# A new source order in a decoder trunk: softmax behind its scores, a projection between scores and scaling, transposes behind the next projection

## The chip, the cores and the metric

The kernel runs on one core of one Trainium2 chip. The metric is the device time of one execution in microseconds, as the median of several runs. The profile shows one execution: TensorE (PE, with its weight loads PEld), VectorE (DVE), ScalarE (ACT), GpSimd (POOL) and the DMA queues, of which SyncE (SP) issues most.

## The reference

A decoder trunk of two layers, 512 tokens of width 1024, all in float32. Layer 0 mixes with a gated DeltaNet (6 heads of 128), layer 1 with sliding-window attention (12 query heads, 2 key heads of width 64, window 128, a sink logit per head). Each layer also attends with 4 heads into 256 fixed memory tokens, and ends in a SwiGLU block of width 2816.

```python
for layer in range(2):
    h = rms_norm(x, ln_mix[layer])
    mem_k, mem_v = split(mem_n @ w_mem_kv[layer])
    if layer == 0:   # q, k, v: projection, causal convolution of 4 taps, SiLU
        mix_out, mem_q = gated_deltanet_mixer(h, ...)
    else:
        proj = h @ swa_w_q
        mix_out = sliding_window_attention(rope(proj[:, :768]), shared_k, shared_v, sinks)
        mem_q = proj[:, 768:]
    mem_o = memory_attention(mem_q, mem_k, mem_v)       # softmax(q k / 8) v
    x = x + concat([mix_out, mem_o]) @ w_out[layer]
    x = x + swiglu(rms_norm(x, ln_ffn[layer]), w_gate_up[layer], w_down[layer])
    if layer == 0: shared_k, shared_v = split(rms_norm(x, ln_kv) @ w_kv)
return rms_norm(x, ln_final)
```

The DeltaNet runs in 4 chunks of 128 tokens here: within a chunk a triangular system is inverted, and a state of 128 x 128 per head is carried from chunk to chunk.

## The kernel before

Activations lie transposed, features on the 128 partitions and 512 tokens along the free axis, in eight tiles. Each float32 operand of a projection is split into a rounded high part and a low rest (`split`, L166: ACT copies `hi`, DVE subtracts to get `lo`), and a projection of 128 outputs (`project`, L199) is 8 x 3 = 24 matmuls of 128 x 512. Its weights are loaded by SP into `wraw` (2 buffers), then split into `whi` on ACT and `wlo` on DVE (3 buffers).

Stages in order: `mem_and_norm` and `gates` (to about 48 us), `gdn` (to about 281 us, with the first output products mixed in), output projection and SwiGLU of layer 0 (to about 660 us), `swa` (to about 781 us), output projection and SwiGLU of layer 1.

The Python source issues the instructions. When the program is built, a planner gives every engine its fixed queue: it works through the program with estimated durations and lets an engine take, among the instructions that it then thinks ready, the one that stands first in the source. So an engine's queue isn't the source order, but the source order decides who goes first; on the chip each engine then works through its queue in order and waits where an input is late. `nosync` (L114) adds an order between two instructions of one engine. `use` (L120) switches ACT's function table (`LN_EXP` for Exp and Ln, `SILU_SIN` for SiLU) behind all users of the former table.

`gdn` (L454): for each of 6 heads, `conv_tile` (L444) projects a key tile into a PSUM bank `pj` (3 banks), ACT copies it with one tap's gain and DVE adds three more taps; then SiLU, 4 transposes on PE into a bank `g`, a copy to `kg` and 4 squares (L473 to L486). Products of keys follow (L502), the gate projections, two memory queries `qm`, and the inversion of 32 x 32 blocks on DVE (`base_inverse`, L613: 31 steps of two operations, `btmp` and `big`). Then two passes (L544): memory attention of one query tile, three query heads projected and convolved, SiLU, products with the keys. Then `solve` (L652), `values` (L562: projection, convolution, SiLU, transposes, per head) and `scan` (L575: four chunks, heads inside; `scan_step`, L678, with PSUM banks `sc`), for heads 0 to 2 and then 3 to 5, and `finish` (L582: norm and gate, which make the operands of the output projection).

Attention: `scores(q, k)` (L710) makes, for two blocks of 128 queries at a time, 8 score matmuls into a bank pair (`qk` in layer 1, one pair), takes maxima on DVE (for windows with the mask, into tiles `sm`), and for memory tiles also the exponentials. `weigh` (L748) computes for windows the exponentials (14 on ACT, L767) with their sums `den`, then the reciprocal (L770), scales the probabilities (`sm`, half of the blocks on ACT, half on DVE), transposes them on PE into `pt` (in layer 0 into `g`), copies them to `pf`, multiplies with the values into `sc`, and splits the result into the operand of the output projection. A `nosync` (L790) puts the first transpose of a tile behind the last score matmul issued before it.

`swa` (L1064) orders 8 tiles, 6 and 7 being memory queries: two projections, keys, values, `score(6)`, then `queries(0)`, `score(7)`, `weigh(6)`, and the loop L1127: next tile's query, this tile's scores, last tile's `weigh`.

Of the kernel before, what the change touches and what calls it, by code (L numbers as in the profile page):

```python
# [9 lines left out]
F32 = mybir.dt.float32  # L10
# [76 lines left out]
class Builder:  # L87
# [366 lines left out]
    def gdn(self, gp):  # L454
# [15 lines left out]
        N = [every[:, h * NC:(h + 1) * NC, :] for h in range(H)]  # L470
        ss = self.t(gp, [P, NH], F32, "ss")
        self.weng = nc.vector
        for h in range(H):  # L473
            k = self.conv_tile(H + h, self.t(gp, [P, T], F32, f"kn{h}"))
            self.fn(k, k, AF.Silu)
            kn.append(k)
            ps = self.bank("g")
            for c in range(NC):
                self.tr(ps[:, chunk(c)], k[:, chunk(c)])
            t = c4(self.t(gp, [P, T], F32, f"kg{h}"))  # L480
            self.copy(t, c4(ps))
# [54 lines left out]
            h, c = divmod(i, NC)  # L536
            self.copy(kg[h][:, c, :], kg[h][:, c, :], scale=f[:, 2, i:i + 1])

        def memory(m):
            self.use(LN_EXP)  # L540
            self.attention(gp, qm[m], self.memK[m], self.memV, m, mq[m])


        for h0 in (0, 3):  # L544
            memory(h0 // 3)
            ts = [self.conv_tile(h, self.t(gp, [P, T], F32, "qv", 5)) for h in range(h0, h0 + 3)]
            self.use(SILU_SIN)
# [12 lines left out]
        vt = []  # L560

        def values(heads):  # L562
            for h in heads:
                v = self.conv_tile(2 * H + h, self.t(gp, [P, T], F32, "qv", 5))
                self.fn(v, v, AF.Silu)
                ps = self.bank("g")
                for c in range(NC):
                    self.tr(ps[:, chunk(c)], v[:, chunk(c)])
                self.tt(nc.vector, N[h], c4(ps), wide(ir[h]), ALU.mult)
                vt.append(N[h])  # L570
# [1 line left out]

        S = [None] * H

        def scan(heads):  # L575
            for c in range(NC):
                for h in heads:
                    S[h] = self.scan_step(gp, h, c, S[h], kn[h], Tt[h], kg[h], vt[h], qg[h], AT[h], br[h])

# [22 lines left out]
        for heads in (first, second):  # L602
            self.solve(gp, heads, [N[h] for h in heads], X, [Tt[h] for h in heads])
        values(first)
        scan(first)
        values(second)
        self.use(LN_EXP)
        scan(second)
        finish(first)
# [94 lines left out]
        return new  # L704


    def attention(self, pool, q, kk, vv, m, out, sinks=None):
        self.weigh(pool, self.scores(pool, q, kk, sinks is not None), vv, m, out, sinks)

    def scores(self, pool, q, kk, win):  # L710

        nc = self.nc
        own = "pt" in self.pbufs
        half = [slice(0, 64), slice(64, P)]
        sm = [self.t(pool, [P, 2, 2, 2 * P], F32, "sm", 4 if own else 2) for _ in range(2)]
        sm = [t[:, n] for t in sm for n in range(2)]
        mx = self.t(pool, [P, 2 * NC], F32, "mx", 2)
        den = self.t(pool, [P, 2 * NC], F32, "den", 2)
        nm = self.t(pool, [P, 2 * NC], F32, "nm", 2)
        for n0 in range(0, NC, 2):  # L720
            if own:
                two = self.bank("qk", [P, 2, 2, 2 * P])
                ps = [two[:, b] for b in range(2)]
            else:
                ps = [self.bank("sc" if n0 else "g", [P, 2, 2 * P]) for _ in range(2)]
            for n in (n0, n0 + 1):
                ks = slice((n - 1) * P if n else 0, (n + 1) * P) if win else slice(0, ML)
                c0 = P if win and n == 0 else 0
                for b in range(2):
                    self.scored = self.mm(ps[b][:, n - n0, c0:], q[half[b], n * P:(n + 1) * P], kk[half[b], ks])  # L730
            for b in range(2):
                i = b * NC + n0
                if win:
                    for n in (n0, n0 + 1):
                        c0 = 0 if n else P
                        nc.vector.tensor_tensor_reduce(  # L736
                            out=sm[n][:, b, c0:], in0=ps[b][:, n - n0, c0:], in1=self.band[:, c0:], scale=1.0,
                            scalar=NEG, op0=ALU.add, op1=ALU.max, accum_out=mx[:, b * NC + n:b * NC + n + 1])
                else:
                    nc.vector.tensor_reduce(out=mx[:, i:i + 2], in_=ps[b], op=ALU.max, axis=AX.X)  # L740
                    self.ts(nm[:, i:i + 2], mx[:, i:i + 2], -0.125, ALU.mult)
                    for n in (n0, n0 + 1):
                        i = b * NC + n
                        self.fn(sm[n][:, b, :], ps[b][:, n - n0, :], AF.Exp, scale=0.125, bias=nm[:, i:i + 1],
                                accum_out=den[:, i:i + 1])
        return sm, mx, den, nm

    def weigh(self, pool, scores, vv, m, out, sinks):  # L748

        nc = self.nc  # L750
        win = sinks is not None
        own = "pt" in self.pbufs
        half = [slice(0, 64), slice(64, P)]
        sm, mx, den, nm = scores
        if win:
            sk = sinks.unsqueeze(2).to_broadcast([P, 2, NC])
# [11 lines left out]
                            accum_out=den[:, i:i + 1])  # L768
            self.tt(nc.vector, den, den, es, ALU.add)
        nc.vector.reciprocal(den, den)  # L770
        o = self.bank("sc")
        group = NC if own else 2
        for n in range(NC):
            if n % group == 0:
                pf = {}
            k0 = 1 if win and n == 0 else 0
            p = sm[n][:, :, k0 * P:]
            dn = den.rearrange("p (b n) -> p n b", b=2)[:, n, :]
            for b in range(2):
                if n % 2:  # L780
                    self.copy(p[:, b], p[:, b], scale=dn[:, b:b + 1])
                else:
                    self.ts(p[:, b], p[:, b], dn[:, b:b + 1], ALU.mult)
            pt = self.bank("pt" if own else "g", [P, 2, 2, P])
            for j in range(k0, 2):
                for b in range(2):
                    turned = self.tr(pt[:, j, b, :], sm[n][:, b, j * P:(j + 1) * P])
                    if own and self.scored is not None:

                        self.nosync(turned, self.scored)  # L790
                        self.scored = None
            pf[n] = self.t(pool, [P, 2, 2, P], F32, "pf", group)
            if own and n == 2:
                nc.vector.tensor_copy(pf[n][:, k0:], pt[:, k0:])
            else:
                self.copy(pf[n][:, k0:], pt[:, k0:])
# [267 lines left out]
    def swa(self, sp):  # L1064
# [41 lines left out]
        def score(t):  # L1106
            got[t] = self.scores(sp, qs[t], kk[0] if t < 6 else memK[t - 6], t < 6)

        def weigh(t):
            mix[t] = self.pair(self.bpool)  # L1110
            if t < 6:
                self.weigh(sp, got[t], vv, t, mix[t], sinks[:, t, :])
            else:
                self.weigh(sp, got[t], memV, t - 6, mix[t], None)

        got = {}
        queries(6)
# [1 line left out]
        keys()  # L1119
        values()  # L1120
        score(6)
        transpose_values()
        queries(0)
        score(7)
        weigh(6)
        last = 7
        for t in range(6):  # L1127
            if t < 5:
                queries(t + 1)
            score(t)  # L1130
            weigh(last)
            last = t
        weigh(last)
        return [mix[t] for t in range(KD)]
# [88 lines left out]
```

## Time and profile before

| | |
|---|---|
| median of 3 runs | 1165.34 us (1165.07 to 1167.91) |
| the profiled execution | 1165.44 us, its span 1163.7 us |
| PE busy | 1139.6 us (98%), 7476 matmuls |
| DVE busy | 843.7 us (73%) |
| ACT busy | 635.8 us (55%) |
| PE in the chain that ended last | 88% |

A row of the timeline has start, duration, engine, line, operation, tile written and tiles read, shape and count; in square brackets the engine's idle time just before and what ended it. A row of the sums has the stretch, its length, busy time and number of instructions of PE, PEld, DVE, ACT and POOL, the granted clock, the busy share of the DMA engines and GB/s; for one tile the engines that don't touch it are left out. Matmuls are pipelined: a record is longer than the distance to the next one's start, so gaps are read from start to start.

### The profile page before, as it was taken

To read this page: it belongs to the slowest core of one execution; us is meant where nothing else is said; L and a number is where in the kernel's file an instruction comes from. 1 tells how busy PE (TensorE), PEld (TensorE's weight loads), DVE (VectorE), ACT (ScalarE), POOL (GpSimd) and SP (SyncE) were. 2 spreads that over 40 slices of the span, in tenths; PEclk is the share of its full clock that TensorE was granted. 3 is DMA by queue.
4 is the path that set the end of the run, shared out by engine and by line. 5 is a ranking of instruction groups with operands and counts; after the bars stand their busy time and mean duration, and the time that the engine had idled before them with its cause. 6 is when DMAs were issued, how large, how long until landed. Compare 5 with 4: busy or idle time off the path is not lost.

```text
span 1163.7 us, 19670 instructions
## 1 busy us (share of the span) xinstructions
PE 1139.6 (98%) x7476; PEld 997.3 (86%) x7476; DVE 843.7 (73%) x1587; ACT 635.8 (55%) x1273; POOL 85.9 (7%) x97
## 2 busy tenths in 40 slices
PE   7999999999999999999999999999999999999996
PEld 6888777877899998899998777678999988999986
DVE  5754877767789887378866767859799843898754
ACT  7569563366556652256654547675566522566533
POOL 0310000000101100011100000010011100111000
PEclk9999999999999999999999999999999999999998
DMA  8434352224657744567723421143477733577232
GB/s 307 135 101 115 113 127 92 74 90 163 170 142 187 183 127 124 148 148 179 182 70 102 136 73 38 55 107 124 106 187 185 186 108 103 141 182 187 70 93 94
DMA packets 73971, 152.83 MB, mean 131 GB/s; under 512 B 17756, under 2 KB 18420, under 8 KB 73876
## 3 DMA queue, kind: packets, MB, share of 16 engines
q1 hardware_dynamic: 62356, 130.59, 36.2%
q0 software_dynamic: 11520, 20.98, 11.7%
q8 instruction: 59, 0.97, 0.4%
q14 instruction: 36, 0.29, 0.1%
HBM read 144.58 MB, written 6.96 MB: 130 GB/s over the span
## 4 chain that ended last, share of the span: by engine, by line
PE 88%; DVE 7%; ACT 2%; DMA 1%; issue 1%; SPq 0%; DVEq 0%; ACTq 0%
PE pj L144 42%; PE g L144 39%; PE sc L144 5%; DVE wlo L151 2%; PE pt L148 1%; PE g L148 1%; ACT whi L138 1%; ACT sm L132 1%; DMA wraw<-in_wmk 1%; DVE sm L736 0%; DVE l L154 0%; DVE l L151 0%; PE qk L144 0%; DMA wraw<-in_win 0%; DVE q L151 0%
## 5 line engine op out<-in xcount | busy, mean ns | idle before, releaser
L138 ACT ACTIVATE whi<-wraw 128x512 fp32r<-128x512 f32 (+2 forms) x331 | 244.9, 746 | 272.5 <-PE pj L144 179.3
L151 DVE TENSOR_TENSOR wlo<-wraw,whi 128x512 fp32r<-128x512 f32 (+2 forms) x331 | 274.1, 837 | 108.3 <-ACT whi L138 102.4
L144 PE MATMUL pj<-h,whi 128*128 128x512 f32 (+1 forms) x676 | 266.1, 395 | 0.2
L144 PE MATMUL pj<-l,whi 128*128 128x512 f32 (+1 forms) x676 | 265.0, 392 | 0.3 <-DVE l L154 0.3
L144 PE MATMUL pj<-h,wlo 128*128 128x512 f32 (+1 forms) x676 | 265.0, 392 | 0.0
L144 PE MATMUL g<-T,whi 128*128 128x256 f32 x1280 | 232.1, 282 | 0.0
L144 PEld LDWEIGHTS g<-T,whi 128*128 128x128 f32 x1280 | 196.8, 189 | 1.5 <-DVE fu L154 1.5
L144 PE MATMUL g<-T,wlo 128*128 128x256 f32 x640 | 180.1, 281 | 0.0
L144 PEld LDWEIGHTS pj<-h,whi 128*128 128x128 f32 x676 | 127.0, 188 | 29.3 <-issue 3.1
L144 PEld LDWEIGHTS pj<-l,whi 128*128 128x128 f32 x676 | 127.0, 188 | 27.5 <-issue 2.0
L144 PEld LDWEIGHTS pj<-h,wlo 128*128 128x128 f32 x676 | 127.2, 188 | 26.6 <-issue 1.9
L144 PE MATMUL g<-h,wlo 128*128 128x256 f32 (+1 forms) x508 | 146.5, 288 | 0.0
L144 PE MATMUL g<-h,whi 128*128 128x256 f32 (+1 forms) x508 | 146.3, 288 | 0.0
L144 PE MATMUL g<-l,whi 128*128 128x256 f32 (+1 forms) x508 | 146.1, 288 | 0.0
L144 PEld LDWEIGHTS g<-T,wlo 128*128 128x128 f32 x640 | 120.4, 188 | 0.0
L144 PEld LDWEIGHTS g<-h,wlo 128*128 128x128 f32 x508 | 96.5, 190 | 1.2 <-issue 0.2
L144 PEld LDWEIGHTS g<-l,whi 128*128 128x128 f32 x508 | 96.5, 190 | 1.3
L144 PEld LDWEIGHTS g<-h,whi 128*128 128x128 f32 x508 | 96.5, 190 | 1.2
L972 POOL DMA_DIRECT2D ws<-in_wgu x40 | 35.6, 890 | 733.5 <-ACT sq L141 246.2
L138 ACT ACTIVATE whi<-ws 128x512 fp32r<-128x512 f32 x80 | 50.5, 631 | 52.6 <-PE g L144 43.2
L151 DVE TENSOR_TENSOR fu<-pj,rstd 128x512 f32<-128x512 f32 (+1 forms) x34 | 22.4, 659 | 55.8 <-PE pj L144 55.7
L151 DVE TENSOR_TENSOR wlo<-ws,whi 128x512 fp32r<-128x512 f32 x80 | 54.8, 685 | 7.3 <-ACT whi L138 7.2
(345 smaller groups left out, 1629.4 us busy)
## 6 DMA issues: line engine op xcount, KB each, us to landing
wraw<-in_wgu SPq DMA_DIRECT2D x48, 512.0 KB, 4.2
ws<-in_wgu SPq DMA_DIRECT2D x80, 256.0 KB, 3.6
ws<-in_wgu POOLq DMA_DIRECT2D x80, 256.0 KB, 4.8
wraw<-in_wdn SPq DMA_DIRECT2D x48, 384.0 KB, 3.2
wraw<-in_win SPq DMA_DIRECT2D x26, 512.0 KB, 3.7
wraw<-in_wgu SPq DMA_DIRECT2D x40, 256.0 KB, 4.3
wraw<-in_wout SPq DMA_DIRECT2D x16, 512.0 KB, 3.6
wraw<-in_wdn SPq DMA_DIRECT2D x16, 256.0 KB, 2.7
```

The costliest lines, as they stand in the source:

```text
L132: ins = self.nc.scalar.activation(out, in_, func, **kw).ins
L138: self.copied = self.nc.scalar.activation(out, in_, AF.Copy, **kw).ins
L144: return self.nc.tensor.matmul(out, lhsT, rhs, start=start, stop=stop, skip_group_check=more).ins
L148: return self.nc.tensor.transpose(out, in_, self.ident[:k, :k]).ins
L151: return eng.tensor_tensor(out=out, in0=a, in1=b, op=op).ins
L972: nc.gpsimd.dma_start(s1, a22, accum_op=ALU.add)
```

## The change

No arithmetic changes. In the DeltaNet layer a key's projection is issued ahead of the former key's transposes, and the same for values; in each memory pass the first query projection stands between the scores and the scaling; the last chunk of the first three heads' scan is issued behind the projection of the other heads' values. In the sliding-window layer `weigh` is divided: `soften` (exponentials, reciprocal, scaling) of a tile is issued behind its scores and the former tile's `weigh`, ahead of the next query projection; the tiles that this keeps alive get more buffers (`sm` 6 instead of 4, `mx`, `den` and `nm` 3 instead of 2).

```diff
-        for h in range(H):
+        def key(h):
             k = self.conv_tile(H + h, self.t(gp, [P, T], F32, f"kn{h}"))
             self.fn(k, k, AF.Silu)
             kn.append(k)
+        key(0)
+        for h in range(H):
+            if h < H - 1:
+                key(h + 1)
+            k = kn[h]
             ps = self.bank("g")
...
-        def memory(m):
+        for h0 in (0, 3):
+            m = h0 // 3
             self.use(LN_EXP)
-            self.attention(gp, qm[m], self.memK[m], self.memV, m, mq[m])
-        for h0 in (0, 3):
-            memory(h0 // 3)
-            ts = [self.conv_tile(h, self.t(gp, [P, T], F32, "qv", 5)) for h in range(h0, h0 + 3)]
+            got = self.scores(gp, qm[m], self.memK[m], False)
+            query = lambda h: self.conv_tile(h, self.t(gp, [P, T], F32, "qv", 5))
+            ts = [query(h0)]
+            self.soften(gp, got, None)
+            self.weigh(gp, got, self.memV, m, mq[m], False)
+            ts += [query(h) for h in (h0 + 1, h0 + 2)]
             self.use(SILU_SIN)
...
         def values(heads):
+            vs = {}
+            def value(h):
+                vs[h] = self.conv_tile(2 * H + h, self.t(gp, [P, T], F32, "qv", 5))
+                self.fn(vs[h], vs[h], AF.Silu)
+            value(heads[0])
             for h in heads:
-                v = self.conv_tile(2 * H + h, self.t(gp, [P, T], F32, "qv", 5))
-                self.fn(v, v, AF.Silu)
+                if h + 1 in heads:
+                    value(h + 1)
+                v = vs[h]
                 ps = self.bank("g")
...
-        def scan(heads):
-            for c in range(NC):
+        def scan(heads, chunks=range(NC)):
+            for c in chunks:
...
         values(first)
-        scan(first)
+        scan(first, range(NC - 1))
         values(second)
+        scan(first, range(NC - 1, NC))
         self.use(LN_EXP)
         scan(second)
...
-        sm = [self.t(pool, [P, 2, 2, 2 * P], F32, "sm", 4 if own else 2) for _ in range(2)]
+        sm = [self.t(pool, [P, 2, 2, 2 * P], F32, "sm", 6 if own else 2) for _ in range(2)]
-        mx = self.t(pool, [P, 2 * NC], F32, "mx", 2)
+        mx = self.t(pool, [P, 2 * NC], F32, "mx", 3 if own else 2)
...
-    def weigh(self, pool, scores, vv, m, out, sinks):
+    def soften(self, pool, scores, sinks):
...
         nc.vector.reciprocal(den, den)
...
                     self.copy(p[:, b], p[:, b], scale=dn[:, b:b + 1])
                 else:
                     self.ts(p[:, b], p[:, b], dn[:, b:b + 1], ALU.mult)
+
+    def weigh(self, pool, scores, vv, m, out, win):
...
         score(6)
+        soften(6)
         transpose_values()
         queries(0)
         score(7)
         weigh(6)
+        soften(7)
         last = 7
         for t in range(6):
             if t < 5:
                 queries(t + 1)
             score(t)
             weigh(last)
+            soften(t)
             last = t
```

More of the change, by code (lines that the diff above doesn't have):

```diff
@@ L704, in scan_step @@
         return new
-    def attention(self, pool, q, kk, vv, m, out, sinks=None):
-        self.weigh(pool, self.scores(pool, q, kk, sinks is not None), vv, m, out, sinks)
     def scores(self, pool, q, kk, win):
@@ L714, in scores @@
         half = [slice(0, 64), slice(64, P)]
-        sm = [self.t(pool, [P, 2, 2, 2 * P], F32, "sm", 4 if own else 2) for _ in range(2)]
+        sm = [self.t(pool, [P, 2, 2, 2 * P], F32, "sm", 6 if own else 2) for _ in range(2)]
         sm = [t[:, n] for t in sm for n in range(2)]
-        mx = self.t(pool, [P, 2 * NC], F32, "mx", 2)
-        den = self.t(pool, [P, 2 * NC], F32, "den", 2)
-        nm = self.t(pool, [P, 2 * NC], F32, "nm", 2)
+        mx = self.t(pool, [P, 2 * NC], F32, "mx", 3 if own else 2)
+        den = self.t(pool, [P, 2 * NC], F32, "den", 3 if own else 2)
+        nm = self.t(pool, [P, 2 * NC], F32, "nm", 3 if own else 2)
         for n0 in range(0, NC, 2):
@@ L746, in scores @@
         return sm, mx, den, nm
-    def weigh(self, pool, scores, vv, m, out, sinks):
+    def soften(self, pool, scores, sinks):
         nc = self.nc
         win = sinks is not None
-        own = "pt" in self.pbufs
-        half = [slice(0, 64), slice(64, P)]
         sm, mx, den, nm = scores
@@ L770, in weigh @@
         nc.vector.reciprocal(den, den)
-        o = self.bank("sc")
-        group = NC if own else 2
         for n in range(NC):
-            if n % group == 0:
-                pf = {}
             k0 = 1 if win and n == 0 else 0
@@ L783, in weigh @@
                     self.ts(p[:, b], p[:, b], dn[:, b:b + 1], ALU.mult)
+    def weigh(self, pool, scores, vv, m, out, win):
+        nc = self.nc
+        own = "pt" in self.pbufs
+        half = [slice(0, 64), slice(64, P)]
+        sm = scores[0]
+        o = self.bank("sc")
+        group = NC if own else 2
+        for n in range(NC):
+            if n % group == 0:
+                pf = {}
+            k0 = 1 if win and n == 0 else 0
             pt = self.bank("pt" if own else "g", [P, 2, 2, P])
@@ L1107, in score, with soften @@
             got[t] = self.scores(sp, qs[t], kk[0] if t < 6 else memK[t - 6], t < 6)
+        def soften(t):
+            self.soften(sp, got[t], sinks[:, t, :] if t < 6 else None)
         def weigh(t):
@@ L1111, in weigh @@
             if t < 6:
-                self.weigh(sp, got[t], vv, t, mix[t], sinks[:, t, :])
+                self.weigh(sp, got[t], vv, t, mix[t], True)
             else:
-                self.weigh(sp, got[t], memV, t - 6, mix[t], None)
+                self.weigh(sp, got[t], memV, t - 6, mix[t], False)
         got = {}
```

## The prediction

> **What bounds the kernel now.** I read first the page's busy times, then the sums of two stretches: the attention stage of layer 1 (662.6 to 781.2 us) and the DeltaNet stage from its first memory scores on (129.5 to 280.8 us).
>
> ```profile
> PE 1139.6 (98%) x7476; PEld 997.3 (86%) x7476; DVE 843.7 (73%) x1587; ACT 635.8 (55%) x1273; POOL 85.9 (7%) x97
> 662.60:781.20 118.60, 115.71 (x769) 87.73 (x769) 80.03 (x248) 75.47 (x216) 3.48 (x4) 1.00 0.24 69
> 129.50:280.78 151.28, 148.14 (x1097) 118.01 (x1097) 111.99 (x235) 83.06 (x172) 0.00 (x0) 1.00 0.31 93
> ```
>
> PE leads everywhere, at the full granted clock (1.00). But its 98% overstates it: a projection's matmul is recorded at 0.39 us, while in an unbroken row they start 0.23 us apart (those at 751.38 and 751.61, quoted below). So I count gaps between starts. The Trainium skill, page "Perfetto Trace Analysis", section "Identifying the Most-Contended Engine", calls matmul busy time a poor measure and takes weight-load busy time instead; the 0.39 us against 0.23 agree with the first half. By the second, 14% of the span (166 us) would be open, which the starts do not bear out.
>
> For the attention stage: matmuls by output tile (pj, g, sc, pt, qk, in this order), and from the timeline how far apart groups start.
>
> ```profile
> 662.60:781.20 118.60, 68.20 (x265) 48.23 (x265) 12.82 (x26) 0.00 (x0) 1.00 0.24 69
> 662.60:781.20 118.60, 7.37 (x28) 4.78 (x28) 0.00 (x0) 1.27 (x2) 1.00 0.24 69
> 662.60:781.20 118.60, 14.80 (x232) 12.46 (x232) 5.50 (x8) 4.67 (x8) 1.00 0.24 69
> 662.60:781.20 118.60, 18.35 (x116) 12.86 (x116) 5.53 (x8) 12.68 (x24) 1.00 0.24 69
> 662.60:781.20 118.60, 17.65 (x128) 10.39 (x128) 21.51 (x56) 8.15 (x32) 1.00 0.24 69
> 697.97 1.13 PE L144 MATMUL qk<-mk,q 64*128 64x256 f32 x8
> 699.03 1.09 PE L148 MATMUL pt<-consts,sm 128*128 128x128 f32 x8
> 699.88 0.48 PE L144 MATMUL pj<-h,whi 128*128 128x512 f32 x1
> 702.36 1.97 PE L144 MATMUL sc<-pf,mv 128*64 128x128 f32 x32
> 704.26 0.93 PE L144 MATMUL qk<-ks,q 64*128 64x128 f32 x8
> ```
>
> Eight qk take 1.06 us, eight pt 0.85, thirty-two sc 1.90. Counting g with pj, the work is 293 x 0.227 = 66.5, 128 x 0.133 = 17.0, 116 x 0.106 = 12.3 and 232 x 0.059 = 13.8, in all 109.6 us of 118.6. About 9 us are gaps: the ceiling here. No PE instruction is added or removed, so the change can only open or close gaps.
>
> **The attention stage (L1106 to L1133).** Where a gap comes from, at one tile:
>
> ```profile
> 749.43 0.19 ACT L132 ACTIVATION_READ_ACCUMULATOR sm<-sm,nm 128x1 f32 x1
> 751.38 0.39 PE L144 MATMUL pj<-l,whi 128*128 128x512 f32 x1
> 751.42 0.42 DVE L736 CUSTOM_DVE_ANT_0 sm<-qk,consts 128x256 f32<-128x256 f32 x1
> 751.61 0.39 PE L144 MATMUL pj<-h,wlo 128*128 128x512 f32 x1
> 751.76 0.16 DVE L151 TENSOR_TENSOR den<-den,es 128x8 f32<-128x8 f32 x1
> 751.84 1.22 DVE L151 TENSOR_TENSOR wlo<-wraw,whi 128x1024 fp32r<-128x1024 f32 x1
> 751.93 1.14 PE L144 MATMUL qk<-ks,q 64*128 64x256 f32 x8
> 752.98 0.19 DVE L770 RECIPROCAL den<-den 128x8 f32<-128x8 f32 x1
> 753.20 0.75 DVE L158 TENSOR_SCALAR sm<-sm,den 128x128 f32<-128x128 f32 x3
> 753.64 0.54 PE L148 MATMUL pt<-consts,sm 128*128 128x128 f32 x3 [0.57 <-DVE sm L158]
> 753.94 0.48 PE L144 MATMUL pj<-h,whi 128*128 128x512 f32 x1
> 754.25 0.52 PE L148 MATMUL pt<-consts,sm 128*128 128x128 f32 x3
> ```
>
> The exponentials of the tile end at 749.6. Its sum `den` runs only at 751.76, behind the next tile's maxima on DVE; then a weight split of 1.22 us goes ahead of the reciprocal. The first scaled probabilities come at about 753.5, and PE, whose eight qk from 751.93 need 1.06 us, starts the transposes at 753.64: 0.65 lost. The same at three other tiles:
>
> ```profile
> 717.07 0.50 PE L144 MATMUL pj<-l,whi 128*128 128x512 f32 x1
> 718.26 0.30 PE L148 MATMUL pt<-consts,sm 128*128 128x128 f32 x1 [0.69 <-DVE sm L158]
> 728.79 1.14 PE L144 MATMUL qk<-ks,q 64*128 64x256 f32 x8
> 730.43 0.54 PE L148 MATMUL pt<-consts,sm 128*128 128x128 f32 x3 [0.51 <-DVE sm L158]
> 741.93 1.13 PE L148 MATMUL pt<-consts,sm 128*128 128x128 f32 x6 [0.28 <-DVE sm L158]
> ```
>
> 1.19 - 0.23 = 0.96; 1.64 - 1.06 = 0.58; and the shown 0.28. Together 2.5 us. With `soften(t)` in the source ahead of the next tile's query and scores, sum, reciprocal and scaling can run from 749.6 on, 1.35 us of DVE (0.16 + 0.19 + four at 0.25), done by about 751.0 plus ACT's four. The first transpose still stands behind the next tile's last score matmul (L790), so it finds its input ready. I take all 2.5. Also, scaled tiles that trickle in split the transposes: a pj between two pt groups costs 0.31 (753.94 to 754.25) instead of 0.23, and the return as much. The timeline of the stage has 26 pt groups from 699.03 on (16 would do, two a tile): 10 x 0.16 = 1.6, half taken, 0.8; the bounds are 0 and 1.6.
>
> What it costs: the 1.35 us stand ahead of the next tile's first maxima, whose bank the second-half qk needs, so that qk may come 1.35 later. Cover: the projection two tiles ahead, from 748.98 on in an unbroken row in this trace. The last tile lacks it, since queries are used up; output products fill instead. I charge 0.5 once, bounds 0 and six tiles x 1.35 = 8.1. The delayed weight split has slack: its weights serve the projection after the one that runs. Two more `sm` and one more of `mx`, `den`, `nm` add no instruction. Term: -2.8 us.
>
> **Memory attention of layer 0 (L539 to L546).**
>
> ```profile
> 120.00:140.00 20.00, 18.40 (x91) 14.45 (x90) 19.25 (x51) 11.26 (x26) 0.00 (x0) 1.00 0.31 103
> 136.60 0.39 PE L144 MATMUL pj<-l,whi 128*128 128x512 f32 x1
> 137.66 0.19 DVE L770 RECIPROCAL den<-den 128x8 f32<-128x8 f32 x1
> 138.59 0.30 PE L148 MATMUL g<-consts,sm 128*128 128x128 f32 x1 [1.60 <-DVE sm L158]
> ```
>
> PE stands 1.99 - 0.23 = 1.76 us: transposes were queued after 23 of the projection's 24 products, and the exponentials ran until 137.6. Now the whole projection, its ACT copy and three DVE taps (0.74 each, below) come first in source, then the scaling; so transposes are queued later, with a second projection's products in between if its weights are split. Bounds: -1.8 if the wait goes; +2.2 for each of two passes if the taps hold the scaling up on DVE (19.25 busy of 20 us here) with PE standing, +4.4. I take -1.0, near the first, because in this trace PE does run on with pj wherever some are queued. The change adds no switch of activation tables. Nothing of SP or POOL is passed: the moved pieces issue only the projection's weight load, and these keep their order.
>
> **Values and scan (L562 to L605), keys (L473).**
>
> ```profile
> 247.07 0.48 PE L144 MATMUL pj<-h,wlo 128*128 128x512 f32 x1
> 247.96 1.22 DVE L151 TENSOR_TENSOR wlo<-wraw,whi 128x1024 fp32r<-128x1024 f32 x1
> 250.81 0.74 DVE L154 SCALAR_TENSOR_TENSOR qv<-pj,gains,qv 128x509 f32<-128x509 f32 x1
> 251.44 0.38 PE L144 MATMUL sc<-DT,vn 128*128 128x128 f32 x2
> 252.71 0.66 PE L148 MATMUL g<-consts,qv 128*128 128x128 f32 x4 [0.89 <-ACT qv L132]
> 60.95 0.66 PE L148 MATMUL g<-consts,kn 128*128 128x128 f32 x4 [0.36 <-ACT kn L132]
> ```
>
> The last value head takes 5.6 us from its last product (247.07) to its transposes; PE runs short at 251.44 and stands 0.89. The held-back last chunk of the first scan, 12 products recorded as pairs (251.44 starts one), is filler there, and head 5's projection comes that much earlier. Against it: `finish(first)` needs that chunk, so its output products come later. Bounds: -1.0 and, if they are missing once in the scan's tail, +1.0. I take -0.6. The other value heads' transposes, and keys after the first, cost no wait in the trace; key 0 loses the 0.36 shown. With key 1's products first that goes if its weights are ready: -0.3, bounds -0.4 and 0. Each key's copy and squares come up to 24 products (5.4 us) later, under the next projection; the last head's chain is unchanged.
>
> **Sum.** The profiled execution took 1165.44, its span 1163.7; the median of the runs is 1165.34, so what holds for the one holds for the other. 1165.4 - 2.8 - 1.0 - 0.6 - 0.3 = 1160.7 us.
>
> **Rivals.** (1) No change: source position decides only among instructions that the build thinks ready, so splits may still go ahead, or a closed gap opens elsewhere. For it: four gaps sit on one DVE chain that keeps all its operations. Against: `den` and reciprocal waited with their inputs there. With the key's 0.3 left: 1165.1. The same page of the Trainium skill, section "Identifying Performance Opportunities", says that improving a kernel generally means improving its most-contended engine; PE's work is not touched here, so by that rule the time stays. The trace agrees for unbroken pj rows, not for the four gaps. (2) Slower: softmax ahead of the maxima delays each second-half qk by 1.35 us, and PE, in order, stands at it. Six tiles, 8.1, less the 2.5 and the other terms' 1.9: 1169.1. It decides once more than 4.4 us of the 8.1 stay uncovered. Against: pj rows are there to be queued ahead of qk. (3) Twice the gain: transposes in one piece throughout, the whole 9 us of gaps and the other terms at their best (1.8 + 1.0 + 0.4): 1153.2. Against: some of the 9 us is the ramp between kinds of matmul.
>
> **How the numbers follow.** Forecast 0.50 (1157.5 to 1163), no change 0.23, slower 0.15, twice the gain 0.12. About 0.3%, 3.5 us, is what a measurement here tells from no change, so 0.05 of the forecast falls within it, as does 0.01 of the slower case: faster 0.57, same 0.29, slower 0.14. The range 1154.5 to 1167.5 leaves out most of the twice-gain case and about two thirds of the slower one.
>
> **What would show it.** Right: PE's waits on the scaled `sm` gone from the attention stage, reciprocal straight behind `den` and ahead of `wlo`, fewer pt groups, the stage 2 to 4 us shorter; the 1.6 us wait near 138 gone; transposes of the last value head without wait. Wrong: waits of qk on DVE maxima, transposes of the first memory pass waiting on DVE taps, or a longer stretch from the last value head to the unbroken output products.

## Result and the profile after

The changed kernel takes 1163.11 us (median of 11 runs, 1162.35 to 1164.21), the kernel before 1166.01 us in the same series (11 runs, 1165.07 to 1167.91): ratio 0.9975, 95% interval 0.9965 to 0.9984, or 2.9 us less (1.9 to 4.1). The two profiled executions differ by 1.2 us only (1165.44 and 1164.21; spans 1163.7 and 1162.4), since the changed one is the longest of its 11 runs and that of before lies below its median. So I read the traces stage by stage, and the medians only for the whole.

The busy times of the changed kernel, and the sums of two stretches, with the columns as before: the attention stage, and the DeltaNet stage from its first memory scores to the unbroken products of layer 0's output projection:

```profile
PE 1139.2 (98%) x7476; PEld 997.1 (86%) x7476; DVE 845.2 (73%) x1587; ACT 634.2 (55%) x1273; POOL 85.9 (7%) x97
661.95:778.83 116.88, 115.29 (x769) 87.85 (x769) 79.47 (x248) 74.83 (x215) 3.51 (x4) 1.00 0.24 69
128.90:283.80 154.90, 151.31 (x1114) 120.57 (x1113) 114.06 (x238) 83.61 (x174) 0.00 (x0) 1.00 0.32 96
```

The second stretch in the kernel before, to the same product (3.6 us further than in the prediction, where the end was taken at products that mix with others):

```profile
129.50:284.42 154.92, 151.78 (x1114) 121.01 (x1113) 115.03 (x239) 85.75 (x175) 0.00 (x0) 1.00 0.33 98
```

The work is the same. The attention stage lost 1.7 us (118.60 to 116.88). The DeltaNet stage is no shorter (154.92 to 154.90): its memory passes, from the first score to the first product of `solve`, take 54.94 us instead of 53.79, and what follows gives 1.2 us back. The first memory score came 0.6 us earlier (129.51 to 128.91); two kernels below whose code up to there is that of before reach it at 128.86 and 128.93, so this need not come from the change. The stretch behind the attention stage took 1.1 us more; the last section comes to that. One tile of the attention stage after, from the timeline (rows of the exponentials, rope and projection left out):

```profile
734.93 0.93 PE L144 MATMUL qk<-ks,q 64*128 64x128 f32 x8
...
736.86 0.17 DVE L151 TENSOR_TENSOR den<-den,es 128x8 f32<-128x8 f32 x1
...
737.15 0.20 DVE L782 RECIPROCAL den<-den 128x8 f32<-128x8 f32 x1
...
737.51 1.69 ACT L138 ACTIVATE sm<-sm,den 128x256 f32<-128x256 f32 x4
737.82 1.01 DVE L158 TENSOR_SCALAR sm<-sm,den 128x128 f32<-128x128 f32 x4
738.74 0.43 DVE L750 CUSTOM_DVE_ANT_0 sm<-qk,consts 128x256 f32<-128x256 f32 x1
...
739.63 1.23 DVE L151 TENSOR_TENSOR wlo<-wraw,whi 128x1024 fp32r<-128x1024 f32 x1
740.11 1.14 PE L144 MATMUL qk<-ks,q 64*128 64x256 f32 x8
...
741.17 1.57 PE L148 MATMUL pt<-consts,sm 128*128 128x128 f32 x10
```

This is the order that was forecast: reciprocal right behind `den`, scaling done by 738.8, weight split behind it, and ten transposes in one group at 741.17 without a wait. PE's waits in this stage, before (first fence) and after (second; engine, line, what it waited for: us in all, times, longest):

```profile
PE pt L148 <- DVE sm L158: 2.0, 4, 0.7
PE qk L144 <- ACT sm L132: 0.5, 1, 0.5
```

```profile
PE pt L148 <- DVE sm L158: 0.5, 1, 0.5
PE qk L144 <- ACT sm L132: 0.5, 1, 0.5
PE pt L148 <- ACT pf L138: 0.3, 1, 0.3
```

The groups of pt went from 26 to 19. In the DeltaNet stage the timeline after has the memory pass and the last value head thus:

```profile
138.30 0.30 PE L148 MATMUL g<-consts,sm 128*128 128x128 f32 x1 [1.69 <-DVE sm L158]
...
249.46 0.39 PE L144 MATMUL sc<-DT,vn 128*128 128x128 f32 x2
249.68 0.63 PE L148 MATMUL g<-consts,qv 128*128 128x128 f32 x4
```

The value head's transposes no longer wait and come 3.0 us earlier (252.71 to 249.68); the wait of the memory pass is still there (1.60 before). And something new, in the chain that ended last after (start, us, what), and among PE's waits from 240 to 290 us, before and after:

```profile
265.49 3.95 DMA kn<-q
270.31 3.03 PE g L144 x6
```

```profile
PE g L148 <- ACT qv L132: 0.9, 1, 0.9
PE g L144 <- DVE N L151: 0.4, 1, 0.4
```

```profile
PE g L144 <- DVE N L151: 0.7, 1, 0.7
PE sc L144 <- ACT gcr L138: 0.3, 1, 0.3
```

`finish` loads copies of the queries into the key buffers `kn`, which the scan reads to its end; so with the scan 2.7 us earlier (last product 271.08 to 268.40) PE's products with a matrix of ones for the output gate (`g<-N,consts`) stand 0.7 us on these loads, through DVE's `N`.

### The profile page after: what moved, and what is told of

Its sections match the earlier page's. It is cut to its first block, busy times and chain, and to the rows that moved or that the text cites. A ratio compares the mean times of both kernels' runs of the same rounds, so it can differ in the third digit from the quotient of the medians.

```text
span 1162.4 us, 19658 instructions
## 1 busy us (share of the span) xinstructions
PE 1139.2 (98%) x7476; PEld 997.1 (86%) x7476; DVE 845.2 (73%) x1587; ACT 634.2 (55%) x1273; POOL 85.9 (7%) x97
## 4 chain that ended last, share of the span: by engine, by line
PE 88%; DVE 6%; ACT 2%; DMA 2%; issue 1%; SPq 0%; DVEq 0%; ACTq 0%
PE pj L144 41%; PE g L144 38%; PE sc L144 6%; DVE wlo L151 1%; PE pt L148 1%; DMA wraw<-in_wout 1%; ACT sm L132 1%; PE g L148 1%; PE qk L144 1%; DVE l L154 1%; DMA wraw<-in_wmk 1%; DVE btmp L151 1%; DVE big L151 0%; ACT whi L138 0%; DMA big<-basein 0%
## 5 line engine op out<-in xcount | busy, mean ns | idle before, releaser
L151 DVE TENSOR_TENSOR fu<-pj,rstd 128x512 f32<-128x512 f32 (+1 forms) x34 | 22.4, 660 | 56.2 <-PE pj L144 56.2
```

Source lines behind the costliest of these rows:

```text
L151: return eng.tensor_tensor(out=out, in0=a, in1=b, op=op).ins
```

## The experiments

My theory: each part's gain is what its own stage shows (attention about 1.3 us, values 1.2, keys 0.3), and the memory part loses about 1 us. The rival: the parts work only together, or the attention gain needs the further buffers. Ratios are to the kernel before in runs on the same chip. There were three series, each on a chip of its own, and the median of the kernel before was 1165.69 us for the four parts alone; 1166.72 us for only the scaling moved, the old buffers, the changed kernel without the memory part, and that with early copies; and 1165.78 us for the other four. So times of different series are compared by their ratios.

**The sliding-window part alone.**

```diff
 # the changed kernel's scores, soften, weigh and swa; layer 0 in the old order, but with
 # weigh split there too
-            self.attention(gp, qm[m], self.memK[m], self.memV, m, mq[m])
+            got = self.scores(gp, qm[m], self.memK[m], False)
+            self.soften(gp, got, None)
+            self.weigh(gp, got, self.memV, m, mq[m], False)
```

> The sliding-window part alone (softening behind the scores, six sm buffers); layer 0 as before. Theory A (the two traces): the attention stage, from the first memory scores to the unbroken output products, gets about 1.7 us shorter, and about 1.0 of it is given back until the second SwiGLU's quarter products, because the output weights land no sooner; time 0.7 to 1.7 us under the kernel before. Theory B (the prediction's term): 2.8 us under it, nothing given back. Layer 0's marks unchanged within 0.1 us in both.

1164.51 us, ratio 0.9990 (0.9982 to 0.9999). From the first score product to the last weighted one the stage takes 95.64 us, as in the changed kernel (95.63; before 96.88). The part stands alone. The time is in Theory A's range, but nothing is given back behind the stage: from there to the first product of `T` in layer 1 it takes 56.72 us, against 56.68 before. Theory A had this step wrong; the last section has what lengthened it in the changed kernel's profile. Layer 0 did not stay within 0.1 us either: from the first memory score to the solve it takes 54.14 us, against 53.79 before.

**Keys alone.**

```diff
+        key(0)
         for h in range(H):
-            k = self.conv_tile(...); self.fn(k, k, AF.Silu)
+            if h < H - 1:
+                key(h + 1)
+            k = kn[h]
```

> The key loop alone. A and B agree on the stretch from the first key transposes to the key products: about 0.3 us shorter. A: what follows in layer 0 shifts by 0.3 as a whole, so the time falls by 0.3 us (not to be told from no change). Rival: layer 0 waits for the block inversion's and the DMAs' chain anyway, and nothing is left at the first output products.

1165.50 us, ratio 0.9999 (0.9990 to 1.0008). In the trace the key loop, from its first transposes to the first product of keys, takes 39.92 us against 40.08 before (39.77 in the changed kernel). A gain of 0.2 or 0.3 us can't be told from none in the time. Over all profiles of this study it is clearer: 40.08 to 40.55 us in the seven kernels without this part, 39.41 to 39.92 in the seven with it.

**The memory part alone.**

```diff
             got = self.scores(gp, qm[m], self.memK[m], False)
+            ts = [query(h0)]
             self.soften(gp, got, None)
             self.weigh(gp, got, self.memV, m, mq[m], False)
-            ts = [query(h) for h in range(h0, h0 + 3)]
+            ts += [query(h) for h in (h0 + 1, h0 + 2)]
 # in the attention stage: old order, soften(last) directly ahead of weigh(last)
```

> The query projection between memory scores and scaling alone (both passes); the rest in the order of before. Theory A: the wait of PE for the first scaled probabilities stays at 1.6 to 1.7 us, and the block solve starts about 1.2 us later than before; time 0.5 to 1.2 us above the kernel before. Theory B (the prediction's term): the wait shrinks and the time falls by 1.0 us. Theory C: the later solve is made up by filler in the scan, and the time stays within 0.3 us.

1166.20 us, ratio 1.0003 (0.9994 to 1.0012). From the first memory score to the solve it takes 54.69 us (before 53.79), and PE's wait near 138 us stays. It was a surprise that its attention stage is 0.86 us shorter (96.02), although the order there is the old one: only the scaling of all blocks stands ahead of the transposes. A later run takes this up. So this kernel is not the memory part alone: the time holds that gain too. It speaks against Theory B's 1.0 us less and does not decide between A and C.

**Values and scan alone.**

```diff
+            value(heads[0])
             for h in heads:
+                if h + 1 in heads:
+                    value(h + 1)
...
-        scan(first)
+        scan(first, range(NC - 1))
         values(second)
+        scan(first, range(NC - 1, NC))
```

> The values' and the scan's order alone. Theory A: the last value head's transposes come about 3 us earlier and the second scan ends about 2.5 to 3.5 us earlier, but the loads of q2 for heads 3 to 5 are issued no earlier and finish waits for them, so that the unbroken output products start only 0.5 to 1.5 us earlier; time lower by as much. Theory B (the prediction's term): 0.6 us. Rival: full 2.5 us or more reach the end.

1164.52 us, ratio 0.9992 (0.9983 to 1.0001). From the solve to the scan's last product 84.35 us against 87.78, but to the first product of the next stage's `T` tiles (SwiGLU of layer 0) 151.21 against 152.63: of 3.4 us won 2.0 seem to be given back behind the scan. This is Theory A's outcome. But part of both numbers is work that moved over the mark: up to the scan's last product PE has 173 products of 128x512 instead of 177, and the four stand behind it. Three of them are in the sums for the output tile pj from the gate's last product to the first of `T` (before, then the changed kernel, which has the same order here):

```profile
274.30:335.93 61.63, 49.79 (x210) 1.00 0.56 161
```

```profile
272.75:335.31 62.56, 51.20 (x213) 1.00 0.54 157
```

At 0.227 us each, the four are 0.9 us. So 2.5 us were won in the scan and 1.1 lost behind it, most of it ahead of the gate's last product (0.9).

**Only the scaling moved, in the attention stage.**

```diff
 # the kernel before; scaling of all four blocks in a loop of its own
+        soften(last)     # exponentials, reciprocal, scaling of all blocks
+        weigh(last)      # transposes, products
-        weigh(last)
```

> The kernel before, with one thing changed: in the attention stage of layer 1 the scaling of a tile's four blocks stands in one piece ahead of all its transposes, where it stood block by block among them; the tile's softmax stays behind the next tile's scores, buffers as before, layer 0 as before. Theory A (the order of soften and scores is what closed the gaps): the stage from the first score product to the last weighted one stays at 96.9 us (within 0.3) and the waits of the transposes on the scaled probabilities stay. Theory B (taking the scaling out of the transposes' loop is most of it, as the run with the memory edit alone hinted, 96.02): 96.0 us, the groups of transposes fewer than before, and the time 0.5 to 1.0 us below the kernel before.

1165.35 us, ratio 0.9990 (0.9981 to 0.9999); the stage 96.04 us. Theory B as far as the length of the stage goes; but pt groups fell from 26 only to 25, the gain sits at one tile, and PE's waits on the scaled probabilities stay (1.8 us in four places, 2.0 before), as Theory A had it.

**The sliding-window part with the old buffers and layer 0 untouched.**

```diff
-        sm = [self.t(pool, [P, 2, 2, 2 * P], F32, "sm", 6 if own else 2) for _ in range(2)]
+        sm = [self.t(pool, [P, 2, 2, 2 * P], F32, "sm", 4 if own else 2) for _ in range(2)]
 # mx, den, nm: 2 each
```

> The sliding-window edit alone, with layer 0 exactly as before and with the buffers of before (four sm, two each of mx, den, nm). If the order is what works, the stage is as in the run with six sm, 95.6 us from first score product to last weighted one, and without that run's 0.2 to 0.35 us loss in layer 0 the time is 1.2 to 1.5 us below the kernel before. If the two further buffers carry the gain (a tile's scores can be evicted while the tile before is still being transposed), the stage goes back to 96.5 us or more, with score products waiting for a free sm.

1164.14 us, ratio 0.9979 (0.9970 to 0.9988); the stage 95.56 us. The further buffers carry nothing of the stage's gain. The time is 2.6 us lower (1.4 to 3.5), more than the 1.2 to 1.5 expected and than the stage shows; where the rest comes from was not found.

**The order without the scaling moved.**

```diff
 # as the run before; the scaling goes back from soften into weigh's loop over blocks
         score(t)
         weigh(last)      # scaling block by block, transposes, products
         soften(t)        # exponentials, den, reciprocal
```

> The counterpart of the run with only the scaling moved: in the attention stage the new order (a tile's denominators and reciprocals behind its own scores, ahead of the next tile's), but the scaling left block by block among the transposes, as before; layer 0 and buffers as before. The kernel with both measures 95.6 us from first score product to last weighted one, the one with the scaling ahead alone 96.0, the kernel before 96.9. Theory A (the two do the same work, each takes away most of it): 95.9 to 96.2 us. Theory B (scaling ahead of the transposes is what counts, the order adds its 0.4 and no more): 96.4 to 96.6 us. Theory C (the order alone gives all): 95.6 us.

1164.41 us, ratio 0.9990 (0.9981 to 0.9999); the stage 94.77 us, lower than any theory had it. The same tile as above, from this kernel's timeline:

```profile
736.01 0.93 PE L144 MATMUL qk<-ks,q 64*128 64x128 f32 x8
...
738.23 0.20 DVE L763 RECIPROCAL den<-den 128x8 f32<-128x8 f32 x1
...
739.79 1.00 DVE L158 TENSOR_SCALAR sm<-sm,den 128x128 f32<-128x128 f32 x4
740.04 1.14 PE L144 MATMUL qk<-ks,q 64*128 64x256 f32 x8
740.72 1.22 DVE L151 TENSOR_TENSOR wlo<-wraw,whi 128x1024 fp32r<-128x1024 f32 x1
741.11 1.57 PE L148 MATMUL pt<-consts,sm 128*128 128x128 f32 x10
```

Here DVE's scaling comes behind the next tile's maxima: the second-half qk starts 4.03 us after the first (736.01 to 740.04) instead of 5.18 (4.24 before), and the transposes still wait for nothing. That looks like 0.9 us more gain, but it is not: in the changed kernel PE fills that time with projection and output products, which must be done in any case. How many stand inside the stage is in its sums for the output tile g, from first score to last weighted product (before, after, scaling alone, order alone):

```profile
678.85:775.73 96.88, 3.15 (x12) 1.00 0.19 52
```

```profile
678.19:773.82 95.63, 3.61 (x14) 1.00 0.19 53
```

```profile
679.31:775.35 96.04, 2.93 (x11) 1.00 0.19 53
```

```profile
679.35:774.12 94.77, 2.08 (x8) 1.00 0.19 54
```

(The columns are the stretch, its length, PE's busy time and count, the granted clock, the busy share of the DMA engines and GB/s.) The matmuls of pj are 187 in each. With the prediction's distances (pj and g 0.227, qk 0.133, pt 0.106, sc 0.059 us) the work of before is 199 x 0.227 + 128 x 0.133 + 116 x 0.106 + 232 x 0.059 = 88.2 us, and PE stood 96.88 - 88.2 = 8.7. In the same way: scaling alone 8.1, order alone 7.5, both 7.0. So the order is worth 1.2 us, the scaling 0.6, both 1.7; they add up, and the stage's end, which I had used as its measure in the expectations, does not show it.

**The changed kernel without the memory part.**

```diff
-            ts = [query(h0)]
-            self.soften(gp, got, None)
-            self.weigh(gp, got, self.memV, m, mq[m], False)
-            ts += [query(h) for h in (h0 + 1, h0 + 2)]
+            self.scale_and_weigh(gp, got, self.memV, m, mq[m], None)   # as before
+            ts = [query(h) for h in range(h0, h0 + 3)]
```

> The changed kernel, with the memory passes of layer 0 put back exactly as they were (scaling block by block, the query projection behind the pass). Theory A (that edit costs 0.6 to 1.0 us of DVE taps ahead of the scaling): first memory score to solve back to 53.8 us from 54.9, and the time 3.3 to 3.9 us below the kernel before. Theory B (the loss there is paid back by the query heads that come earlier): the sum from the first memory score to the first quarter product stays within 0.3 us, and the time is that of the changed kernel, 2.9 us below.

1162.17 us (5 runs, 1161.85 to 1164.24), ratio 0.9967 (0.9955 to 0.9980): near Theory A. First memory score to solve 54.07 us against 54.94 with the part. Kernels with the old form differ here as well, 53.8 to 54.4 us in seven profiles and 55.5 in one; those with one projection moved have 54.65, 54.69 and 54.94. So the part costs some 0.6 us, and nothing shows a gain. It also puts layer 0's scaling in one piece; that alone, in the sliding-window kernel, has 54.14 us, inside the range of the old form.

**Two projections moved, on the changed kernel.**

```diff
-            ts = [query(h0)]
+            ts = [query(h0), query(h0 + 1)]
...
-            ts += [query(h) for h in (h0 + 1, h0 + 2)]
+            ts += [query(h0 + 2)]
```

> The changed kernel with two query projections, not one, between the memory scores and the scaling in layer 0. Theory A (transposes are queued behind more products, so that PE never stands at them): PE's wait of 1.7 us on the scaled probabilities near 138 us goes, first memory score to solve 53.3 us or less (54.9 with one projection, 53.8 with none). Theory B (the second projection's weights are split on ACT only behind the exponentials, and six taps of 0.74 us each now stand ahead of the scaling on DVE): the wait stays or grows, and the stretch is 55 to 58 us.

1163.15 us, ratio 0.9977 (0.9968 to 0.9985), the time of the changed kernel; the stretch 54.29 us. From its timeline:

```profile
141.82 1.03 PE L148 MATMUL g<-consts,sm 128*128 128x128 f32 x8
144.90 1.15 PE L144 MATMUL sc<-pf,mv 128*64 128x128 f32 x16 [1.57 <-ACT pf L138]
```

The wait on the probabilities goes, as Theory A has it, and comes back as 1.57 us at the next step, where PE needs `pf` from ACT. The stretch is what neither theory had (53.3 or less, 55 to 58).

**The same without DVE's taps in the way**, on the kernel without the memory part and with early loads (below).

```diff
+            ts = [self.t(gp, [P, T], F32, "qv", 5) for _ in range(2)]
+            ps = [self.conv_start(h0 + i, t) for i, t in enumerate(ts)]   # products, ACT copy
             self.scale_and_weigh(gp, got, self.memV, m, mq[m], None)
+            for i, t in enumerate(ts):
+                self.conv_taps(h0 + i, t, ps[i])                          # DVE
... # the third query as before; conv_tile divided into conv_start and conv_taps
```

> The kernel with the memory edit undone and the query copies loaded early (1161.3 us), with two query projections' products and ACT copies between the memory scores and the scaling of layer 0, and their DVE taps behind the memory pass. If DVE's taps were what made the memory edit lose, this gains what was hoped from it: the 1.6 us wait near 138 goes and the time falls 1 us or more below 1161.3. If the split of the second projection's weights on ACT behind the exponentials is what PE lacks, the wait stays and the time is within 0.5 us of 1161.3 or above it.

1162.58 us (8 runs), ratio 0.9974 (0.9964 to 0.9984), against 0.9955 (0.9943 to 0.9968) of the kernel that it starts from: no gain, and likely a loss. The wait moves in the same way and is longer (2.09 us at the same instruction), the stretch is 54.81 us against 53.79 there. With the taps out of the way nothing is won, so my explanation by DVE fell.

**Early query copies, on the changed kernel.**

```diff
-                t = self.t(gp, [P, T], F32, f"kn{h}")
+                t = self.t(gp, [P, T], F32, "qv", 5)
                 nc.sync.dma_start(t, q2[h])
```

> The changed kernel with the query copies for layer 0's output gate loaded into the projection's buffers, so that the loads do not wait for the scan. Theory A (these loads are where the scan's gain is given back): last scan product to last ones-product of the gate back from 4.35 us to 3.2, the time 1 us or more below the changed kernel. Theory B (the two earlier runs that differ in this alone stood 3.85 and 3.55 us): 0.3 to 0.5 us in this stretch and in the time, and the 0.9 us between the last ones-product and the first quarter product stay, because the output gate's chain on DVE ends there now.

1163.10 us, ratio 0.9974 (0.9965 to 0.9983). SP's queue and PE after the scan:

```profile
250.32 0.79 SPq L603 DMA_DIRECT2D qv<-q  x2
...
269.52 3.03 PE L144 MATMUL g<-N,consts 128*128 128x512 f32 x6
```

The loads go at 250.3 instead of 265.5 and the products of the gate run 0.8 us earlier without a wait; from the scan's last product to the last of them 3.58 us (4.35 after, 3.22 before). The stretch lies between the two theories. In it one more product of 128x512 stands than before (9 instead of 8), so little is left to win. From there to the first product of `T` it takes 62.55 us against 61.63 before, as Theory B had it, but not for its reason: 0.7 of the 0.9 us are the three products counted above. From `solve` to the first product of `T`: 150.71 us, 0.75 less than after. The time doesn't show it.

**Both: no memory part, early copies.**

> The kernel of the run before this one with one thing more: the query copies that the output gate of layer 0 reads are loaded into the projection's own buffers instead of the key buffers, so that these loads need not wait for the scan's last readers. Theory A (the gain of the scan's new order is given back at these loads): the loads are issued while the scan runs, the wait of 3.95 us on them is gone from the chain, and the time is 4.5 to 5.5 us below the kernel before. Theory B (the loads hide, the next work on DVE sets the end anyway): less than 0.4 us off the run with only the memory edit undone.

1161.28 us (5 runs, 1161.18 to 1161.64), ratio 0.9955 (0.9943 to 0.9968), the fastest here: 5.4 us under its kernel before, against 2.9 for the changed kernel. From 240 to 290 us PE has one wait left:

```profile
PE sc L144 <- ACT gcr L138: 0.3, 1, 0.3
```

The early loads are worth 0.33 us here, from the solve to the first product of `T` (150.79 to 150.46); that is Theory B's outcome. The medians of the pair differ by 0.9 us, and all five runs of this kernel lie below the five of the other, while the intervals of the two ratios overlap; 0.46 us of the profiles' difference lies behind the attention stage (56.61 against 56.15 us), long after these loads. This kernel with the order-only form of the attention stage was not run.

## Why the prediction was right or wrong

The forecast of 1160.7 us was right in sign and too large: 2.9 us instead of 4.7; the measured 1163.11 us lies inside the stated range and just outside the 1157.5 to 1163 that went with the forecast's chance of 0.50. In part that is luck: the memory term was wrong by 1.7 us and the attention term by 1.1, and the values gave 0.7 more than I had taken, which hides some of it. By its steps:

**Attention stage, -2.8: mechanism right, size off; -1.7.** The reciprocal, the splits and the groups came as forecast. Mis-sized is the 2.5 for four waits. I had taken the wait before 718.26 (0.96 us) with the others "the same", without its exponentials. They are in the trace of before:

```profile
717.16 0.19 ACT L132 ACTIVATION_READ_ACCUMULATOR sm<-sm,nm 128x1 f32 x1
717.38 0.17 DVE L151 TENSOR_TENSOR den<-den,es 128x8 f32<-128x8 f32 x1 [1.64 <-ACT sm L132]
```

They end at 717.35 and `den` follows at once; ACT decides there, and after the change 0.81 us of that wait are still there (pj at 716.41, pt at 717.46). At the last tile but one a new wait of 0.54 comes up (761.83 to 762.60, less 0.23), where `den` again follows the exponentials directly; what ends it is ACT's copy `pf`, which stands behind the tile's four scalings there. So 1.7 us of waits went, 0.5 came. The groups were sized right: 7 fewer at 0.16 are 1.1, I had taken 0.8. The 0.5 for a later second-half qk is not seen as a wait; PE filled with 18 pj between the two halves. These readings sum to -2.3; the count of PE's standing time says -1.7, and I have not traced the 0.6 between.

**Memory part, -1.0: wrong.** Measured +0.6 to +0.9. The step that failed is "I take -1.0, near the first, because in this trace PE does run on with pj wherever some are queued": in before 23 of the 24 products already stood ahead of these transposes, so moving the projection in the source gained one product of cover. The runs with two projections show that more cover only moves the wait to `pf`: the chain from exponentials to weighted values sets this pass, and PE's products are used up somewhere along it. What the extra 0.6 us is, stays open. The DVE taps, which I had named as the price, can't be shown to be it: without them two projections lose as well. The traces point to ACT: with one projection moved, ACT's copy of it (0.67 us, at 139.00 in the changed kernel) stands between the first and the other three of its four scalings, where before it came behind all four, and the first weighted products come 12.3 to 12.6 us after the first score instead of 11.3 to 11.9 (12.8 in the key kernel). No run moves this copy alone.

**Values and scan, -0.6: right sign, mis-sized; -1.2 to -1.4.** With the filler that moved taken off, about 2.4 us were won up to the scan's last product and 1.1 lost behind it. The mis-sized step is the bound of -1.0, taken from the one wait of 0.89 us; the transposes of the last value head come 3.0 us earlier. The prediction had bounded the loss in the scan's tail by 1.0 and named `finish(first)` for it. That was near in size, but early loads show 0.3 to 0.75 us of it to be the query copies. The stretch from the last value head's transposes to the unbroken output products, which the prediction named as a sign of being wrong if it grew, grew from 31.7 to 34.1 us: the head came early and the end did not follow as far.

**Keys, -0.3: right** in the trace (0.2 to 0.3 from one pair of profiles, 0.6 between the means of seven and seven; the wait of 0.36 us is down to 0.04, with the keys alone to 0.20). But the wait was not key 0's, as the prediction read it. The transposes at 60.95 are the second group; the first stands at 56.72 without a wait, among later products. What covers the wait now is three more projection products ahead of the second group (17 instead of 14).

Sum of the traces: -1.7 + 0.7 - 1.3 - 0.3 = -2.6, against -2.9 (1.9 to 4.1) measured.

**Rivals.** No change: false. The order of the source did change DVE's queue, as the tile above shows. The Trainium skill, "Perfetto Trace Analysis", section "Identifying Performance Opportunities", says that a kernel is generally improved by improving its most-contended engine, and PE's work is untouched; here PE's busy time is the same (1139.6 and 1139.2 us) and 2.9 us went all the same, since they were time in which PE stood. So the sentence doesn't forecast "no change", as the prediction took it to: closing the time in which that engine stands improves it too. Slower through a late second-half qk: its delay is real, 5.18 us between the halves against 4.24 before and 4.03 with the scaling left in place. PE had 18 projection products for it, and no qk that waits on DVE is among the waits shown above, so it did not decide. Twice the gain: the waits at tiles where ACT's exponentials decide, and 7.0 of 8.7 us that PE still stands, show why not.

## What to carry to other kernels

Before adding up waits of one kind, look at each for what comes last in its chain: of four that looked alike, one hung on the exponentials and stayed. Measure a stage by the time that its bound engine stands, not by its last instruction, when filler work may slide over its end; this happened in both layers here. Work brought forward hits the next dependence: here loads into a buffer that the scan still read, and another buffer let them go earlier.

## What was not expected of the hardware

The third load of output weights behind the attention stage (512 KB) took 3.48 to 3.73 us from issue to landing in ten profiles of this study and 4.38 to 4.71 in the other four. The changed kernel's profile is one of these; its chain has the first and the third load:

```profile
778.85 6.38 DMA wraw<-in_wout
787.65 4.38 DMA wraw<-in_wout
```

Where it took over 4.3 us, the stretch from the last weighted product to the first product of `T` in layer 1 took 57.3 to 57.8 us, else 56.2 to 57.1, and 57.5 in the order-alone kernel, which has three to six more output products in it. The key-alone kernel, whose code here is that of before, is among the four (57.78 against 56.68), so the change is not the cause. So a difference under 1 us over this stretch can't be read from one execution each.
